# The rest of a weight block: a negated copy and an adding transfer in place of a subtraction

## The chip, the cores and the metric

The kernel runs on one core of a Trainium2 chip. The metric is the device time of one execution in microseconds (us), as the median of the runs shown. The core's engines are named as the profile names them: PE is TensorE (matrix products; PEld is its weight load), ACT is ScalarE, DVE is VectorE, POOL is GpSimd, and SP is SyncE, which here only issues transfers. SBUF is the on-chip memory, PSUM the eight banks that matrix products accumulate in, HBM the main memory.

## The reference

One layer of a hybrid decoder on 512 tokens of width 1024, in float32: a short convolution branch and a gated delta rule run side by side and are merged, then comes a gated feed-forward part with a convolution. Cut to what matters here, it is a row of products with large weight matrices, with cheap work on vectors between them:

```python
h = rmsnorm(x, norm_mix_g)
proj = h @ w_in                                   # 1024 x 9232
bg, cg, xv, q, k, v, z, a, b, ga, gb = split(proj)
y_a = (bg * causal_dwconv(cg * xv, conv_a_w)) @ w_a_out
y_b = gdn_branch(q, k, v, z, a, b, ...) @ w_b_out # chunked gated delta rule, 8 heads
x = x + (sigmoid(ga) * y_a + sigmoid(gb) * y_b) @ w_o
h = rmsnorm(x, norm_ffn_g)
up = causal_dwconv(h @ w_up, ffn_conv_w)          # 1024 x 5632
gate, val = split(up)
x = x + (silu(gate) * val) @ w_down               # 2816 x 1024
return rmsnorm(x, norm_final_g)
```

## The kernel before, in words

**Products in two parts.** Every float32 operand of a large product is split into a rounded part in the format float32r ("high", `wh` for weights) and the rest ("low", `wl`), which is the operand minus its rounded part. A product is then three products in float32r: high by high, high by low, low by high. `mm3` (L112) issues the three for the eight 128-row pieces of an input: in the kernel before, first `wh` by the input's low part and `wl` by its high part in turn, and the eight of high by high last. `row_jobs` (L912) does the same for `w_o` and `w_down`, where tokens lie on the output's partitions; there the order within each 128-row piece is low input by `wh`, high input by `wl`, high by high.

**Blocks and jobs.** All weights come as 81 blocks of 1 MB: 128 partitions by 8 pieces of 256 columns (`cols`), or by 2 rows of 1024 columns (`rows`, for `w_o` and `w_down`). A `Block` (L122) has three tiles from the pool `wp`, each in two buffers: `raw`, which `load` fills with one transfer that SP issues (L131), and `wh` and `wl`, which `split` makes. In the kernel before `split` works in pieces of 128 x 512: ACT copies a piece of `raw` into `wh` (L143), and DVE subtracts `wh` from `raw` into `wl` (L144); four pieces make a block.

**Order of the work.** `run_jobs` (L148) walks a list of jobs, one a block. While the products of job i are written out, the split of block i + 1 stands in the queue `splits`; `tick` (called after every four products of 512 columns) takes a step of it and of the queues `chains`, `mids`, `backs` (the stages of the delta rule) and `evacs` (what takes results out of PSUM). Block i + 2 is loaded meanwhile. A new `wh` or `wl` needs the buffer of the block two before, so it can't be written until the last product that reads that one. The framework then sets the order on each engine, and inserts the waits.

**The list.** 16 jobs for q, k, v and z of four pairs of heads, with the delta rule between their products; 4 for gb; 12 for cg, xv and bg; 4 for ga; 4 of `w_a_out`; 4 of `w_b_out`; 4 of `w_o`; 22 of `w_up`; 11 of `w_down`. A job of 256 columns is 48 products of 512 columns. In `row_jobs` the last two blocks are used together: the last but one is used for one or two of the four token groups alone, the rest waits for the last block. The first two blocks of `w_up` are used together as well (`first_val`), by halves of the tokens, in products of 256 columns; before them `fin1` forms the norm (with a power on POOL, L979) and PE turns the result.

**POOL** has little to do in the kernel before: constants, the polynomial of the decay gates (L426 to L443), powers (`sk` L511, `fac` L724, `r` L979 and L1075), a mask of the decay matrix (`Dm` L393), a product with a mask (`um` L538) and copies (`TTf` L616). It runs in order, as every engine does.

## Time and profile before

| | |
|---|---|
| runs shown | 1001.76, 1000.38, 999.54 us; median 1000.38 us |
| profiled execution, first to last instruction (span) | 998.5 us |
| median less span | 1.9 us |
| granted TensorE clock, mean | 0.999 |
| instructions in the span | 14009 |

The profiled execution has its span alone as its own time; the runs also count what lies ahead of the first and behind the last instruction, and the median is 1.9 us above this span. Rows of the trace give the start in us from the span's start, the duration, the engine, the line of the kernel, the operation, output and inputs, and a count where rows were merged; in square brackets stands how long the engine had been idle and who ended it. Products are pipelined: each one is shown for some 0.39 us, and the next one starts 0.23 us after it. A group's row gives busy time, mean duration in ns, and the idle time ahead of it.

### The profile page before, as it was taken

To read this page: it belongs to the slowest core of one execution; us is meant where nothing else is said; L and a number is where in the kernel's file an instruction comes from. 1 tells how busy PE (TensorE), PEld (TensorE's weight loads), DVE (VectorE), ACT (ScalarE), POOL (GpSimd) and SP (SyncE) were. 2 spreads that over 40 slices of the span, in tenths; PEclk is the share of its full clock that TensorE was granted. 3 is DMA by queue.
4 is the path that set the end of the run, shared out by engine and by line. 5 is a ranking of instruction groups with operands and counts; after the bars stand their busy time and mean duration, and the time that the engine had idled before them with its cause. 6 is when DMAs were issued, how large, how long until landed. Compare 5 with 4: busy or idle time off the path is not lost.

```text
span 998.5 us, 14009 instructions
## 1 busy us (share of the span) xinstructions
PE 986.6 (99%) x5602; PEld 822.5 (82%) x5602; DVE 545.8 (55%) x1090; ACT 426.2 (43%) x931; POOL 64.3 (6%) x101
## 2 busy tenths in 40 slices
PE   8999999999999999999999999999999999999997
PEld 5887888888888888888888888988888888888886
DVE  6777776897434434542253553675665666532235
ACT  6695666665353322322331232454444444421123
POOL 3331201202010000000000000000000000000000
PEclk9999999999999999999999999999999999999999
DMA  7343232232212232223223252332223223223212
GB/s 223 105 133 94 72 93 86 72 93 57 88 44 85 85 119 93 85 87 124 85 88 124 85 190 84 106 117 96 85 90 121 85 86 126 85 87 124 84 43 85
DMA packets 95409, 97.60 MB, mean 98 GB/s; under 512 B 20299, under 2 KB 88176, under 8 KB 95344
## 3 DMA queue, kind: packets, MB, share of 16 engines
q1 hardware_dynamic: 95344, 96.70, 30.3%
q8 instruction: 44, 0.72, 0.3%
q14 instruction: 21, 0.17, 0.1%
HBM read 93.27 MB, written 3.42 MB: 97 GB/s over the span
## 4 chain that ended last, share of the span: by engine, by line
PE 96%; DVE 1%; issue 1%; ACT 1%; DMA 0%; SPq 0%; POOL 0%; POOLq 0%; ACTq 0%
PE ps L104 88%; PE ps L484 1%; PE ps L519 1%; PE ps L713 1%; PE ps L693 1%; PE ps L702 1%; PE ps L681 1%; PE ps L680 1%; PE ps L656 0%; PE ps L650 0%; DMA raw<-in_w_in_dram 0%; PE ps L991 0%; ACT hT L341 0%; PE ps L603 0%; PE ps L594 0%
## 5 line engine op out<-in xcount | busy, mean ns | idle before, releaser
L104 PE MATMUL ps<-hT,wh 128*128 128x512 f32 (+1 forms) x1184 | 371.2, 391 | 0.3 <-ACT wh L143 0.3
L144 DVE TENSOR_TENSOR wl<-raw,wh 128x512 fp32r<-128x512 f32 x324 | 211.7, 692 | 160.5 <-ACT wh L143 160.1
L104 PEld LDWEIGHTS ps<-hT,wh 128*128 128x128 f32 x1184 | 218.0, 188 | 41.1 <-ACT wh L143 0.6
L143 ACT CAST wh<-raw 128x512 fp32r<-128x512 f32 x324 | 178.6, 618 | 170.5 <-PE ps L104 162.3
L104 PE MATMUL ps<-hT,wl 128*128 128x512 f32 (+1 forms) x592 | 227.0, 385 | 0.3 <-DVE wl L144 0.3
L104 PE MATMUL ps<-h,wh 128*128 128x512 f32 (+1 forms) x768 | 220.8, 372 | 0.0
L104 PEld LDWEIGHTS ps<-h,wh 128*128 128x128 f32 x768 | 140.1, 188 | 24.9
L104 PE MATMUL ps<-h,wl 128*128 128x512 f32 (+1 forms) x384 | 140.2, 371 | 0.0
L104 PEld LDWEIGHTS ps<-hT,wl 128*128 128x128 f32 x592 | 111.4, 188 | 20.5 <-DVE wl L144 0.5
L104 PE MATMUL ps<-wh,aT 128*128 128x512 f32 x352 | 108.5, 389 | 0.0
L104 PEld LDWEIGHTS ps<-h,wl 128*128 128x128 f32 x384 | 72.3, 188 | 12.5
L104 PEld LDWEIGHTS ps<-wh,aT 128*128 128x128 f32 x352 | 66.1, 188 | 13.7
L104 PE MATMUL ps<-wl,aT 128*128 128x512 f32 x176 | 68.5, 389 | 0.0
L188 DVE SCALAR_TENSOR_TENSOR cv<-ps,wA,cv 128x511 f32<-128x511 f32 (+2 forms) x72 | 53.5, 743 | 11.2 <-ACT cv L185 10.4
L188 DVE SCALAR_TENSOR_TENSOR g<-ps,wF,g 128x511 f32<-128x511 f32 (+1 forms) x44 | 32.9, 747 | 48.2 <-ACT g L185 47.9
L188 DVE SCALAR_TENSOR_TENSOR v<-ps,wF,v 128x511 f32<-128x511 f32 (+1 forms) x44 | 32.8, 747 | 34.6 <-ACT v L185 34.3
L104 PE MATMUL ps<-wh,mix 128*128 128x512 f32 x128 | 40.1, 391 | 0.0
L104 PE MATMUL ps<-ya,wh 128*128 128x512 f32 x128 | 39.6, 389 | 0.0
L104 PE MATMUL ps<-yb,wh 128*128 128x512 f32 x128 | 39.6, 389 | 0.0
L104 PEld LDWEIGHTS ps<-wl,aT 128*128 128x128 f32 x176 | 33.0, 188 | 6.9
L185 ACT ACTIVATE g<-ps,wF 128x512 f32<-128x512 f32 x22 | 15.2, 690 | 38.9 <-PE ps L104 38.9
L185 ACT ACTIVATE v<-ps,wF 128x512 f32<-128x512 f32 x22 | 15.2, 690 | 38.6 <-PE ps L104 38.6
(227 smaller groups left out, 970.0 us busy)
## 6 DMA issues: line engine op xcount, KB each, us to landing
raw<-in_w_in_dram SPq DMA_DIRECT2D x36, 1024.0 KB, 5.1
raw<-in_w_up_dram SPq DMA_DIRECT2D x22, 1024.0 KB, 5.1
raw<-in_w_down_dram SPq DMA_DIRECT2D x11, 1024.0 KB, 4.9
raw<-in_w_a_out_dram SPq DMA_DIRECT2D x4, 1024.0 KB, 5.7
raw<-in_w_b_out_dram SPq DMA_DIRECT2D x4, 1024.0 KB, 5.6
raw<-in_w_o_dram SPq DMA_DIRECT2D x4, 1024.0 KB, 6.7
Dm<-gtd SPq DMA_DIRECT2D x4, 512.0 KB, 3.9
x<-in_x_dram SPq DMA_DIRECT2D x4, 512.0 KB, 6.8
```

Of the source, the lines that this page charges most:

```text
L104: pe.matmul(o, lhsT=a, rhs=b, start=start, stop=stop)
L143: act.copy(out=self.wh[sl], in_=self.raw[sl])
L144: dve.tensor_tensor(out=self.wl[sl], in0=self.raw[sl], in1=self.wh[sl].bitcast(F32), op=ALU.subtract)
L185: act.activation(out=dst, in_=src, func=AF.Copy, scale=wcol(taps - 1))
L188: dve.scalar_tensor_tensor(out=dst[:, sh:], in0=src[:, :S - sh], scalar=wcol(j), in1=dst[:, sh:], op0=ALU.mult, op1=ALU.add)
L484: pe.transpose(out=o[:, n * P:(n + 1) * P], in_=src[:, n * P:(n + 1) * P], identity=ident)
L519: pe.matmul(o[:, i], lhsT=kqs[:, a, h, 0, sl], rhs=kqs[:, b, h, :, sl], start=a > 0, stop=a + b == 0)
L680: pe.matmul(o[:, 0:P], lhsT=kq[:, h, 0, sl], rhs=St[h], start=True, stop=True)
L681: pe.matmul(o[:, P:2 * P], lhsT=kq[:, h, 1, sl], rhs=St[h], start=True, stop=True)
L693: pe.matmul(o[:, 0:P], lhsT=TTf[:, f, :], rhs=rs[h], start=True, stop=True)
L702: pe.matmul(o2[:, 0:P], lhsT=kn[:, f, :], rhs=vns[h], start=True, stop=True)
L713: pe.matmul(o[:, 0:P], lhsT=A[:, f, :], rhs=vns[h], start=True, stop=True)
```

## The change

`split` makes two pieces of 128 x 1024 a block. For the first two blocks (`here`) it still subtracts on DVE. For the other 79, ACT copies the piece into `wh`, then writes minus `wh` into `wl` (L148), and POOL issues a transfer (L149) that reads the piece of the weight from HBM a second time and adds it onto `wl` in SBUF. These are 158 transfers of 512 KB. `mm3` and `row_jobs` issue what needs `wl` last, and `run_jobs` drains the queue `splits` ahead of the call that finishes a block's split, not behind it. Comments were taken out, so lines behind L143 shift by up to four (L393 is L396, L538 is L541, L724 is L727).

```diff
     def mm3(o, pairs, order=KO):
         n = len(pairs)
         pairs = [pairs[k] for k in order]
         for i, (ah, al, bh, bl) in enumerate(pairs):
-            mm(o, ah, bl, i == 0, False)
-            mm(o, al, bh, False, False)
+            mm(o, ah, bh, i == 0, False)
+        for ah, al, bh, bl in pairs:
+            mm(o, ah, bl, False, False)
         for i, (ah, al, bh, bl) in enumerate(pairs):
-            mm(o, ah, bh, False, i == n - 1)
+            mm(o, al, bh, False, i == n - 1)
...
-        def split(self):
+        def split(self, here=False):
             a, b = self.a, self.b
             if self.wh is not None:
                 return
             self.wh = wp.tile([P, a, b], F32R, tag="wh", name=nm("wh"))
             self.wl = wp.tile([P, a, b], F32R, tag="wl", name=nm("wl"))
-            h = max(1, 512 // b)
-            for a0 in range(0, a, h):
-                for b0 in range(0, b, 512):
-                    sl = (slice(None), slice(a0, min(a, a0 + h)), slice(b0, min(b, b0 + 512)))
-                    act.copy(out=self.wh[sl], in_=self.raw[sl])
+            for a0 in range(0, a, a // 2):
+                sl = (slice(None), slice(a0, a0 + a // 2))
+                act.copy(out=self.wh[sl], in_=self.raw[sl])
+                if here:
                     dve.tensor_tensor(out=self.wl[sl], in0=self.raw[sl], in1=self.wh[sl].bitcast(F32),
                                       op=ALU.subtract)
-                    yield
+                else:
+                    act.mul(out=self.wl[sl], in_=self.wh[sl].bitcast(F32), mul=-1.0)
+                    nc.gpsimd.dma_start(out=self.wl[sl], in_=self.src()[sl], accum_op=ALU.add)
+                yield

     def run_jobs(jobs):
         jobs[1][0].load()
         for i, (block, use) in enumerate(jobs):
+            drain(splits)
             Task(block.split()).finish()
-            drain(splits)
             if i + 1 < len(jobs):
-                splits.append(Task(jobs[i + 1][0].split()))
+                splits.append(Task(jobs[i + 1][0].split(i == 0)))
...
-            ks = Task(k_block.split())
+            ks = Task(k_block.split(True))
             norm_x(2)
             ks.step()
             scale_x(2)
             norm_x(3)
-            ks.step()
             scale_x(3)
             ks.finish()
...
-                for kk in range(2):
-                    k = 2 * g + kk
-                    xh, xl = x_[0][:, k, ts_], x_[1][:, k, ts_]
-                    mm(acc[t][hf], xl, wh[:, kk, hs], k == 0, False)
-                    mm(acc[t][hf], xh, wl[:, kk, hs], False, False)
-                    mm(acc[t][hf], xh, wh[:, kk, hs], False, k == nk - 1)
+                xs_ = [(kk, x_[0][:, 2 * g + kk, ts_], x_[1][:, 2 * g + kk, ts_]) for kk in range(2)]
+                for kk, xh, xl in xs_:
+                    mm(acc[t][hf], xh, wh[:, kk, hs], 2 * g + kk == 0, False)
+                    mm(acc[t][hf], xl, wh[:, kk, hs], False, False)
+                for kk, xh, xl in xs_:
+                    mm(acc[t][hf], xh, wl[:, kk, hs], False, 2 * g + kk == nk - 1)
```

Three places show what moves. Behind each name stands the number that the program gives a buffer. The first is POOL's order from the end of the gate polynomial (`g`) to the second mask of the decay matrix, before:

```order
L443 TENSOR_SCALAR g_420<-g_420 128x32 [waits Pool_49]
L511 TENSOR_TENSOR sk_644<-sk_644,phalf 128x8 [waits DVE_49]
L393 AFFINE_SELECT Dm_627<-Dm_627 128x1024 [waits DMAHW2_49]
L538 TENSOR_TENSOR um_755<-U_645,mask_106 32x256 [waits DVE_49]
L393 AFFINE_SELECT Dm_766<-Dm_766 128x1024 [waits DVE_49,DMAHW7_49,Activation_49,Pool_49]
```

And the same stretch now, from `g` on:

```order
L446 TENSOR_SCALAR g_414<-g_414 128x32 [waits Pool_49]
L149 DMA wl_500<-in_w_in_dram 128x4x256 [waits PE_49,Activation_49]
L149 DMA wl_500<-in_w_in_dram 128x4x256 [waits Activation_49]
L149 DMA wl_576<-in_w_in_dram 128x4x256 [waits PE_49,Activation_49]
L149 DMA wl_576<-in_w_in_dram 128x4x256 [waits Activation_49]
L396 AFFINE_SELECT Dm_617<-Dm_617 128x1024 [waits DMAHW2_49]
L514 TENSOR_TENSOR sk_634<-sk_634,phalf 128x8 [waits DVE_49]
L149 DMA wl_778<-in_w_in_dram 128x4x256 [waits DMASW0_49,DMASW1_49,PE_49,Activation_49]
L149 DMA wl_778<-in_w_in_dram 128x4x256 [waits Activation_49]
L541 TENSOR_TENSOR um_743<-U_635,mask_106 32x256 [waits DVE_49]
```

The adding transfers for the third and fourth job (`wl_500`, `wl_576`) stand behind the gate polynomial, and the mask product `um` and later masks stand behind those for the fifth.

The second place is ACT between the third job (v of the first pair) and the fourth (z): the eight sums of squares that become `ssk` (L504, now L507), before:

```order
L504 ACTIVATE junk_642,ssk_640<-ps_647 128x128 [waits PE_49]
L185 ACTIVATE cv_682<-ps_576,wA 128x512 [waits PE_49]
L504 ACTIVATE junk_642,ssk_640<-ps_647 128x128 [waits Activation_49] x3
L504 ACTIVATE junk_642,ssk_640<-ps_667 128x128 [waits PE_49,Activation_49]
L504 ACTIVATE junk_642,ssk_640<-ps_667 128x128 [waits Activation_49] x3
L766 ACT_TABLE_LOAD
L766 ACTIVATE vT_704<-cv_682 128x512 [waits DVE_49]
```

And now, where the exponentials of the decay matrix (`Dm`), a table load, the values (`vT`) and an evacuation (`cv_773`) stand among them:

```order
L507 ACTIVATE junk_632,ssk_630<-ps_637 128x128 [waits Activation_49] x3
L507 ACTIVATE junk_632,ssk_630<-ps_655 128x128 [waits PE_49,Activation_49]
L404 ACTIVATE Dm_617<-Dm_617,negG 128x128 [waits Pool_49]
L404 ACTIVATE Dm_617<-Dm_617,negG 128x128 x7
L507 ACTIVATE junk_632,ssk_630<-ps_655 128x128 [waits Activation_49]
L769 ACT_TABLE_LOAD
L769 ACTIVATE vT_692<-cv_670 128x512 [waits DVE_49]
L507 ACTIVATE junk_632,ssk_630<-ps_655 128x128 [waits Activation_49]
L189 ACTIVATE cv_773<-ps_660,wA 128x512 [waits PE_49]
L507 ACTIVATE junk_632,ssk_630<-ps_655 128x128 [waits Activation_49]
```

The last sum of squares has moved from ahead of the values to behind the evacuation of the third job's second half.

The third place is PE at the start of a block of `w_down` (`aT` is its input), before, where the second product reads `wl`:

```order
L104 MATMUL ps_7513<-wh_7645,aT_5905 128x512 [waits Activation_49]
L104 MATMUL ps_7513<-wl_7646,aT_5904 128x512 [waits DVE_49]
L104 MATMUL ps_7513<-wh_7645,aT_5904 128x512
L104 MATMUL ps_7513<-wh_7645,aT_5905 128x512 [waits Activation_49]
L104 MATMUL ps_7513<-wl_7646,aT_5904 128x512 [waits DVE_49]
```

And now:

```order
L104 MATMUL ps_7367<-wh_7843,aT_5798 128x512 [waits Activation_49]
L104 MATMUL ps_7367<-wh_7843,aT_5799 128x512
L104 MATMUL ps_7367<-wh_7843,aT_5798 128x512 [waits Activation_49]
L104 MATMUL ps_7367<-wh_7843,aT_5799 128x512
L104 MATMUL ps_7367<-wl_7844,aT_5798 128x512 [waits DMASW2_49]
L104 MATMUL ps_7367<-wl_7844,aT_5798 128x512 [waits DMASW3_49]
```

The fifth and sixth product now wait for the two adding transfers, four products (some 0.9 us) into the block. In a block of 256 columns it is the 17th and the 19th.

## The prediction

> **What bounds the kernel now.** I read the page first, its busy times, its chain and its groups:
>
> ```profile
> span 998.5 us, 14009 instructions
> PE 986.6 (99%) x5602; PEld 822.5 (82%) x5602; DVE 545.8 (55%) x1090; ACT 426.2 (43%) x931; POOL 64.3 (6%) x101
> ...
> PE 96%; DVE 1%; issue 1%; ACT 1%; DMA 0%; SPq 0%; POOL 0%; POOLq 0%; ACTq 0%
> ...
> L144 DVE TENSOR_TENSOR wl<-raw,wh 128x512 fp32r<-128x512 f32 x324 | 211.7, 692 | 160.5 <-ACT wh L143 160.1
> ...
> L143 ACT CAST wh<-raw 128x512 fp32r<-128x512 f32 x324 | 178.6, 618 | 170.5 <-PE ps L104 162.3
> ```
>
> PE is busy 99% of the span and 96% of the chain is PE. DVE's 211.7 us of subtractions, which the change removes, lie beside it; ACT waits 162.3 us for PE to free `wh`. Then the chain in order of time; its longest unbroken stretch but one is
>
> ```profile
> 316.16 303.79 PE ps L104 x1340
> ```
>
> 303.79 / 1340 = 0.227 us a product, so a job of 48 takes 10.9 us. No product is removed; the pace stays. A gain can come only from places where PE idles, a loss only where the new `wl` comes too late.
>
> Next the transfers:
>
> ```profile
> q1 hardware_dynamic: 95344, 96.70, 30.3%
> raw<-in_w_down_dram SPq DMA_DIRECT2D x11, 1024.0 KB, 4.9
> Dm<-gtd SPq DMA_DIRECT2D x4, 512.0 KB, 3.9
> x<-in_x_dram SPq DMA_DIRECT2D x4, 512.0 KB, 6.8
> ```
>
> 30.3% of 998.5 us for 96.70 MB is 3.13 us of all 16 DMA engines per MB, or 3.28 us for a block of 1024 KB.
>
> **The change part by part.**
>
> *DVE, ACT, POOL in total.* DVE loses 324 subtractions (211.7 us) and gets four of twice the size back, some 5 us. On ACT a row of a `w_down` block shows four casts in 2.19 us:
>
> ```profile
> 905.01 2.19 ACT L143 CAST wh<-raw 128x512 fp32r<-128x512 f32 x4 [8.70 <-PE ps L104]
> 905.67 2.50 DVE L144 TENSOR_TENSOR wl<-raw,wh 128x512 fp32r<-128x512 f32 x4 [8.38 <-ACT wh L143]
> 908.20 11.25 SPq L131 DMA_DIRECT2D raw<-in_w_down_dram  x2
> ```
>
> That is 0.53 us from start to start, so 1.06 us for a piece of 1024, and I price the negation alike: 4.2 us a block for 2.2, or about 165 us more, 59% of the span. PE hides that, save where ACT is full (below). POOL gets 158 issues. The shared DMA engines carry 79 blocks more: 79 x 3.28 = 259 us (26% of the span) if an add costs what a plain transfer does, 52% if it costs double, since it must also read what it adds to.
>
> *An add of 512 KB.* No trace of before shows one. To landing: at least 3.9 us (the 512 KB row), at most 6.8 (the other one); I take 5.1, between them, near a plain 1024 KB. In DMA engine time: 1.64 us at plain price, 3.28 at double. A speed below the plain one has no reason here, so no gain lies in it.
>
> *Start.* The first block's pieces are twice as large, and DVE scales `x` behind the first of them:
>
> ```profile
> 14.02 0.67 ACT wh L143
> 14.71 0.03 DVE wl L144
> 14.75 0.57 issue
> 15.32 0.75 DVE xr L326
> 16.22 0.41 PE ps L331 x2
> ```
>
> The cast grows by 0.5 us and the subtraction by 0.6; DVE waited little of it before, so the turn at 16.22 us comes about **0.9 us later**, and all behind it. The high products that now come first don't help: only four stand ahead of the turn.
>
> *Third job.* Its adds stand on POOL behind the gate polynomial:
>
> ```profile
> 39.36 0.29 POOL L443 TENSOR_SCALAR g<-g 128x32 f32<-128x32 f32 x1
> 45.40 0.14 PE ps L447 x2
> ```
>
> L447 stands 12 products into the job, and `wl` is wanted 4 products and 0.9 us of small ones later, at 47.2 us. The start shifts both POOL's end and this alike. From 39.65 to 47.2 are 7.6 us for the first add; the second has 8.0 and shares the engines. With 5.1 us for one and 3.3 more for the other it lands 8.4 us on: **0.3 us** late (0 to 1.6).
>
> *ACT from 45 to 70 us.* The window, then three rows of it:
>
> ```profile
> 50.00:75.00 25.00, 25.00 (x131) 21.10 (x130) 19.35 (x57) 23.43 (x65) 8.82 (x7) 1.00 0.44 133
> 47.45 1.28 ACT L455 ACT_TABLE_LOAD   x1
> 57.16 2.46 ACT L401 ACTIVATE Dm<-Dm,negG 128x128 f32<-128x128 f32 x8 [0.68 <-POOL Dm L393]
> 60.14 0.60 PE L484 MATMUL ps<-ident,kq 128*128 128x128 f32 x4
> ```
>
> ACT is busy 23.43 of 25 us, with 2 us a block to come. In the new order it has, from the third job's start (45.40 less 12 products, 0.9 later: 43.6): a cast and `kqs` 1.4, an evacuation 0.7, two negations 2.1, three table loads 3.8 among small work of 1.7: 53.3. Then sums and an evacuation, 2.6; `Dm` 2.46; a table load 1.28, `vT` 0.6, an evacuation 0.7 and three sums 1.4: the last sum of squares ends at about 62.3. `kn` (L505, 0.7) waits for it: 63.0. It frees the bank for PE's second turn in the fourth job, which stood at 60.14 and now comes 0.9 and six products later, at 62.4: **0.6 us** (0 to 2). On POOL `um` waits behind the adds, which wait for ACT's negations; nobody wants it for some 25 us.
>
> *The one stall of before.* DVE was late for `fac`:
>
> ```profile
> 195.24 1.64 POOL L724 TENSOR_TENSOR fac<-fac,nhalf 128x8 f32<-128x8 f32 x1 [7.89 <-DVE fac L723]
> 197.25 0.53 PE L484 MATMUL ps<-ident,vs 128*128 128x128 f32 x2 [0.74 <-DVE vs L732]
> ```
>
> With DVE freed it goes, with the products' hidden latency: **-0.9 us**; the product stream is next.
>
> *Blocks of `w_o` and `w_down`.* `wl` is wanted in the fifth product. Counted at 905 us: `wh` is free two products earlier than before (904.6), two casts and a negation end at 907.8, the second at 908.8; the next `raw` leaves at 906.7, when the casts end (SP waited for the subtraction before, to 908.20). Landing takes 4.9 us, 1.6 over its 3.28 of engine time; so the engines end both adds at 906.7 + 1.6 + 3.28 + 2w = 911.6 + 2w, and PE wants them at 905.0 + 10.9 + 0.9 = 916.8. It holds to w = 2.6; at 3.28 each block is 1.4 us late. I take 0.2 for each of 13 blocks: **2.6 us** (0 to 18).
>
> *The last block of each.* It has less time, as the job ahead is short. In `w_down`:
>
> ```profile
> 970.29 2.18 ACT L143 CAST wh<-raw 128x512 fp32r<-128x512 f32 x4 [8.70 <-PE ps L104]
> ```
>
> The order lets PE run 27 products (6.1 us) before `wl`; the first add leaves 2.9 us in, and with 3.9 to 5.1 lands at 6.8 to 8.0: 1.3 us. In `w_o`, 28 products (6.3): 1.2. Together **2.5 us** (1 to 5).
>
> *From `w_o` to `w_up`.*
>
> ```profile
> 623.69 2.19 ACT L143 CAST wh<-raw 128x512 fp32r<-128x512 f32 x4 [1.31 <-PE ps L104]
> 629.82 0.28 PE L104 MATMUL ps<-h,wh 128*128 128x256 f32 x1
> 629.94 0.28 PE L104 MATMUL ps<-h,wl 128*128 128x256 f32 x1
> ```
>
> From the cast to the first product are 6.1 us, then 16 narrow products of 0.12: `wl` is wanted 8.0 us in. Casts and a negation take 3.2, the add 5.1: 8.3; the second half, `w_up`'s second and third blocks the like. **2.0 us** (0 to 3.5). POOL's powers for the norm (L979) stand among these adds, which could delay PE's turns too.
>
> *Elsewhere* a block of 256 columns has `wl` wanted 16 products in: the second negation ends some 3 us into the job ahead, the add has over 11 us. That slack hides it; without it each job would grow.
>
> The sum: 0.9 + 0.3 + 0.6 - 0.9 + 2.6 + 2.5 + 2.0 = **+8.0 us**. Against its own time, the span, that is 1006.5; the median of the runs lies 1.9 us above the span: 1000.4 + 8.0 = **1008.4 us**. With the low ends 1001.4, with the high ends 1031.
>
> **A rule of the Trainium skill against it.** The row above gives 3.28 us for a block moved once. The Trainium skill's page Collectives: The Full Stack, section The bandwidth ceiling: the fold count and why AG ≠ RS ≠ AR, says that an add in the DMA costs two source reads, and so about halves the rate; no run of before can show it here. By that rule w is 3.28, the row blocks cost 18.2 us in place of 2.6, and the sum would be +23.6, or 1024.0 us, still inside this case.
>
> **The rivals.**
>
> *No net change.* If adds cost the plain 1.64 us and land in 3.9, only the start and the last blocks remain, and the freed DVE pays for them: within 2 us, 1000.4. For it: PE's 99% and 11 us of slack in most jobs. Against: the short windows above, which need no slow add.
>
> *Faster.* DVE is the mechanism, in the first 225 us: if its freed time (over 10% of each 25 us) removes more than the one stall, for PE also idles 0.3 to 0.7 us at waits in the start and loses some 1.7 us around 189 to 200. All of it gone gives 2.7 us: 997.7. It decides once adds land in under 4 us and ACT keeps up; ACT's 23.43 of 25 us speaks against it.
>
> *The adds set the pace.* A wide job lasts 10.9 us, its `raw` takes 3.28 of the engines, so at more than 3.8 us an add (2.3 times plain), or 5.4 us of POOL for an issue, every one of the 65 jobs behind the delta rule grows. At 2.5 times 11.5 us a job, +39: 1039; at three times +144: 1145. For it: an add reads, reads and writes, and POOL's price of an issue stands in no row. Against: DMA engines idle at 70% now.
>
> **How the numbers follow.** The forecast case (late at named places, 1002.4 to 1031) gets 0.52, no change 0.20, faster 0.08, the adds as the pace 0.20. About 2 us (0.2%) is what a measurement of this kernel can tell from no change. So faster 0.08, same 0.20, slower 0.72. The range runs from 998 to 1045: below it 0.05 is left out, above it about 0.13, the pace case's worse part.
>
> **What would show it.** Right: PE idle before `wl` with an add's landing as the reason, at 47, 590, 630 and 970 us and in `w_down`'s blocks; none in the jobs of 316 to 550 us; landings of 4 to 7 us; DVE near 340 us busy, ACT near 590; the turn at 17.1 us. Wrong: every job longer than 10.9 us (the pace), or no wait for `wl` anywhere and a span under 1000.

## The result, and the profile after

The changed kernel takes 1059.37 us (median of 4 runs, 1056.15 to 1061.97) against 1000.01 us before (4 runs, 999.54 to 1001.76): a ratio of 1.0588, 95% interval 1.0565 to 1.0611. It is slower, as forecast, but by 59 us in place of 8, and outside the range. The profiled execution has a span of 1054.4 us, 55.9 more than before; its mean granted clock is 0.977.

The page of the kernel after: span and busy times, the queues, the chain, two of the new groups, and one kind of new transfer.

```profile
span 1054.4 us, 14068 instructions
PE 1006.0 (95%) x5602; PEld 833.5 (79%) x5602; DVE 357.6 (34%) x770; ACT 557.3 (53%) x927; POOL 248.1 (24%) x259
...
q0 software_dynamic: 71904, 82.85, 48.8%
q1 hardware_dynamic: 95344, 96.70, 29.5%
...
PE 74%; DMA 12%; DVE 4%; issue 4%; ACT 3%; POOL 1%; SPq 1%; POOLq 0%; ACTq 0%; DVEq 0%
...
L148 ACT ACTIVATE wl<-wh 128x1024 fp32r<-128x1024 f32 x158 | 159.5, 1050 | 0.0
...
L149 POOL DMA_DIRECT2D wl<-in_w_in_dram x68 | 88.4, 1391 | 237.1 <-ACT wl L148 214.6
...
wl<-in_w_in_dram POOLq DMA_DIRECT2D x68, 512.0 KB, 7.4
```

PE's share of the chain fell from 96% to 74%, and 12% of it is now DMA. The software queue's packets took 48.8% of 1054.4 us for 158 adds, 3.26 us each, 1.9 times what half a block of `raw` takes (29.5% for 96.70 MB is 3.22 us per MB, 1.69 for 512 KB): near the upper of the two bounds in the prediction (3.28). The packets of the adds overlap, as the rates at e8 show, and by those rates an add takes less. An add from `w_in` lands 7.4 us after its issue (median), later than the longest landing assumed (6.8).

What PE waited for, by releaser (total us, times, longest):

```profile
PE ps L597 <- DMA T<-tbd: 12.2, 2, 10.0
PE ps L104 <- DMA wl<-in_w_o_dram: 6.6, 2, 3.6
PE ps L104 <- DMA wl<-in_w_up_dram: 5.2, 3, 2.0
PE ps L104 <- DMA wl<-in_w_down_dram: 4.4, 5, 2.3
PE ps L487 <- DVE kn L508: 3.3, 1, 3.3
```

The longest wait is for a tile that the change doesn't touch: `T`, the inverse factors in the delta rule. Before, no wait for it stood among PE's waits. The second row to the fourth are the waits for `wl` that were forecast.

Where the time went is read from landmarks, the starts of the first products of a kind in the trace (us). Runs e2, e3 and e12 are explained below; they belong in one table.

| stage (from, to) | before | after | e2: adds from block 16 | e3: adds in the middle | e12: mended |
|---|---|---|---|---|---|
| start, to the product on `g` (L447, now L450) | 45.2 | 47.1 | 46.8 | 46.2 | 48.2 |
| delta rule and on: from there to the first product on `ya` | 452.2 | 479.0 | 463.3 | 462.9 | 456.7 |
| `w_a_out` and `w_b_out`: `ya` to `mix` | 87.0 | 87.0 | 87.1 | 87.0 | 87.1 |
| `w_o`: `mix` to `h` | 45.4 | 57.1 | 57.3 | 45.4 | 45.4 |
| `w_up`: `h` to `aT` | 242.4 | 251.1 | 251.2 | 242.4 | 242.3 |
| `w_down`: first to last product of `wh` on `aT` | 119.4 | 125.8 | 126.7 | 119.0 | 119.0 |

So 26.8 us were lost between the start and `ya`, 11.7 in `w_o`, 8.7 at the handover to `w_up` and in its first blocks, 6.4 in `w_down`, and nothing in the jobs between. The start lost 1.9 us here; but among profiled executions of the kernels below whose code is the same up to there this landmark lies anywhere from 45.7 to 49.3 us, so that a single one tells it to a few us only.

### The profile page after: what moved, and what is told of

It is laid out like the page before. It is cut to its first block, busy times and chain, and to the rows that moved or that the text cites. A ratio compares the mean times of both kernels' runs of the same rounds, so it can differ in the third digit from the quotient of the medians.

```text
span 1054.4 us, 14068 instructions
## 1 busy us (share of the span) xinstructions
PE 1006.0 (95%) x5602; PEld 833.5 (79%) x5602; DVE 357.6 (34%) x770; ACT 557.3 (53%) x927; POOL 248.1 (24%) x259
## 3 DMA queue, kind: packets, MB, share of 16 engines
q0 software_dynamic: 71904, 82.85, 48.8%
q1 hardware_dynamic: 95344, 96.70, 29.5%
## 4 chain that ended last, share of the span: by engine, by line
PE 74%; DMA 12%; DVE 4%; issue 4%; ACT 3%; POOL 1%; SPq 1%; POOLq 0%; ACTq 0%; DVEq 0%
PE ps L104 68%; DMA wl<-in_w_down_dram 3%; DMA wl<-in_w_o_dram 2%; DMA wl<-in_w_up_dram 2%; DVE cv L192 1%; DMA Dm<-gtd 1%; ACT wh L143 1%; DMA T<-tbd 1%; PE ps L522 1%; PE ps L487 1%; DMA ucd<-U 1%; ACT wl L148 1%; DMA xt<-in_x_dram 1%; DMA UB<-ucd 1%; DMA tbd<-TB 1%
## 5 line engine op out<-in xcount | busy, mean ns | idle before, releaser
L104 PE MATMUL ps<-hT,wh 128*128 128x512 f32 (+1 forms) x1184 | 291.7, 393 | 1.7 <-ACT wh L143 1.4
L143 ACT CAST wh<-raw 128x1024 fp32r<-128x1024 f32 x162 | 163.1, 1050 | 194.2 <-PE ps L104 192.8
L104 PE MATMUL ps<-h,wh 128*128 128x512 f32 (+1 forms) x768 | 170.4, 375 | 0.0
L148 ACT ACTIVATE wl<-wh 128x1024 fp32r<-128x1024 f32 x158 | 159.5, 1050 | 0.0
L104 PE MATMUL ps<-hT,wl 128*128 128x512 f32 (+1 forms) x592 | 149.8, 393 | 0.0
L149 POOL DMA_DIRECT2D wl<-in_w_in_dram x68 | 88.4, 1391 | 237.1 <-ACT wl L148 214.6
L149 POOL DMA_DIRECT2D wl<-in_w_up_dram x44 | 57.2, 1472 | 180.1 <-ACT wl L148 179.9
L104 PE MATMUL ps<-h,wl 128*128 128x512 f32 (+1 forms) x384 | 89.3, 374 | 5.2 <-DMA wl<-in_w_up_dram 5.2
L104 PE MATMUL ps<-wh,aT 128*128 128x512 f32 x352 | 94.1, 390 | 0.0
L104 PE MATMUL ps<-wl,aT 128*128 128x512 f32 x176 | 55.9, 395 | 4.5 <-DMA wl<-in_w_down_dram 4.4
L192 DVE SCALAR_TENSOR_TENSOR cv<-ps,wA,cv 128x511 f32<-128x511 f32 (+2 forms) x72 | 53.5, 742 | 18.9 <-ACT cv L189 17.9
L192 DVE SCALAR_TENSOR_TENSOR v<-ps,wF,v 128x511 f32<-128x511 f32 (+1 forms) x44 | 32.9, 749 | 57.8 <-ACT v L189 57.1
L149 POOL DMA_DIRECT2D wl<-in_w_down_dram x22 | 18.9, 868 | 103.8 <-ACT wl L148 103.0
```

Source lines behind the costliest of these rows:

```text
L104: pe.matmul(o, lhsT=a, rhs=b, start=start, stop=stop)
L143: act.copy(out=self.wh[sl], in_=self.raw[sl])
L148: act.mul(out=self.wl[sl], in_=self.wh[sl].bitcast(F32), mul=-1.0)
L149: nc.gpsimd.dma_start(out=self.wl[sl], in_=self.src()[sl], accum_op=ALU.add)
L192: dve.scalar_tensor_tensor(out=dst[:, sh:], in0=src[:, :S - sh], scalar=wcol(j), in1=dst[:, sh:], op0=ALU.mult, op1=ALU.add)
```

## The experiments

"e1" means the run whose label begins so. The ratios are to the kernel before.

### Where the loss lies: e1 to e4

Each changes only which blocks are subtracted by DVE (`here`):

```diff
-                splits.append(Task(jobs[i + 1][0].split(i == 0)))
+                splits.append(Task(jobs[i + 1][0].split(True)))        # e1
+                splits.append(Task(jobs[i + 1][0].split(i < 15)))      # e2
+                ... not (16 <= i + 1 < 44 or 51 <= i + 1 < 70) ...     # e3
+                ... i == 0 or i >= 15 ...                              # e4
```

> All 81 blocks get their rest by DVE's subtraction, in two pieces of 128x1024, in the new order of products; no adding transfer and no negation is left. Theory (the adding transfers make the loss): within 2 us of the kernel before, 999 to 1003 us. Rival (the new order of products and the larger pieces make a part of it): over 1006 us, and the delta-rule stage longer than before without any add. DVE then does 162 subtractions of some 1.3 us, about as busy as before.

> Blocks 1 to 15 (the delta rule's jobs) by DVE's subtraction, blocks 16 to 80 by the adding transfer. Theory (the loss is made stage by stage: 28.7 us up to the end of the delta rule, 11.7 in w_o, 8.7 at the handover to w_up, 6.4 in w_down): 1000.0 + 26.8 = 1027 us, 1024 to 1032. Rival (the later stages' lateness depends on the first, or the loss of the first stage comes back later): under 1018 or over 1040.

> Adding transfers only in the column jobs away from the delta rule and the row blocks: blocks 16 to 43 and 51 to 69 (47 of 81 blocks); the others by DVE's subtraction. Theory (a column job wants the rest 16 products in, and that slack hides the add): within 4 us of the kernel before, 998 to 1004. Rival (every add costs something, such as by shared DMA engines or ACT's negations): 47/79 of the 59 us, so 1035; by half of that 1017.

> Adding transfers only for blocks 2 to 15, in the delta rule's stage (28 adds); all others by DVE's subtraction. Theory: 1000.0 + 28.7 = 1029 us, 1022 to 1032, with the landmark at which the first long unbroken stretch of products starts near 344 us. Rival (the loss in the first 345 us comes from the new order of products and piece sizes, not from the adds): near 1000 to 1006.

| run | us, median | ratio, 95% interval |
|---|---|---|
| e1, no add | 1014.69 | 1.0139, 1.0121 to 1.0157 |
| e2, adds from block 16 | 1041.63 | 1.0402, 1.0385 to 1.0418 |
| e3, 47 adding blocks in the middle | 1013.09 | 1.0119, 1.0102 to 1.0137 |
| e4, adds in the delta rule's jobs | 1028.08 | 1.0278, 1.0253 to 1.0303 |

The theory failed for e1: without any add the kernel is 13.2 us slower than before (1014.69 - 1001.51, the median before in that series). e2 and e3 missed their expected times by some 13 us, which they didn't reckon with, and e4 met its own only by luck: 28.7 us were expected of its adds, and 13.2 of them are there without any. Against e1 the parts add up: late adds +26.9 (e2), adds in the delta rule's jobs +13.4 (e4), the middle -1.6, inside the intervals (e3). 13.2 + 26.9 + 13.4 = 53.5 of the 59; the other 6 weren't traced. In the middle an add is indeed free: no stage of e3 behind the start is longer than in e1.

### The 13 us without any add: e5, e11, e13, e9

In e1 PE waits for `T` too, and the rows of the trace show why it is late. Here ACT and DVE in e1:

```profile
56.18 2.44 ACT L404 ACTIVATE Dm<-Dm,negG 128x128 f32<-128x128 f32 x8
...
58.89 1.28 ACT L769 ACT_TABLE_LOAD   x1
...
60.72 0.26 ACT L507 ACTIVATE junk<-ps 128x128 f32<-128x128 f32 x1
...
61.10 0.69 DVE L508 TENSOR_TENSOR kn<-ps,kdv 128x512 f32<-128x512 f32 x1 [1.33 <-ACT junk L507]
```

Before, ACT ended its sums of squares at 53.1 us, and `Dm`'s exponentials came behind them. In e1 the framework put the exponentials, a table load and the values `vT` ahead of the last sums, and `U`, which needs both, starts at 64.4 us, not 57.6. From there the chain `ucd`, `UB`, `TB`, `tbd`, `T` goes on late, and its steps on DVE now stand between the next pair's convolutions: from the first to the end of the last they take 16.8 us (74.0 to 90.8), 8.2 before (68.9 to 77.1). So `T` is issued at 94.84 us, not 79.63. The waits of e1:

```profile
PE ps L597 <- DMA T<-tbd: 4.3, 4, 3.5
PE ps L606 <- DVE TT L590: 1.8, 1, 1.8
```

e5 takes e1 and cuts the split in four pieces again, so that only the order of products is new (and, in the start, one step of the second block's split fewer ahead of the last scaling). e11 takes the kernel before and makes only its pieces larger. e13 is e1 with `T` used later in PE's queue, e9 is e1 with PE's wait filled:

```diff
-            for a0 in range(0, a, a // 2):                              # e5: e1 with
+            h = max(1, 512 // b)
+            for a0, b0 in [(a0, b0) for a0 in range(0, a, h) for b0 in range(0, b, 512)]:
...
-            h = max(1, 512 // b)                                        # e11: before with
-            for a0 in range(0, a, h):
-                for b0 in range(0, b, 512):
+            for a0 in range(0, a, a // 2):
...
-        for _ in range(Y_T):                                            # e13: e1 with
+        for _ in range(Y_T + (8 if pr == 0 else 0)):
...
         o = bank()                                                      # e9: e1 with
+        for _ in range(16 if pr == 0 else 0):
+            pe.matmul(o, lhsT=hT[0][:, 0, 0:P], rhs=hT[0][:, 0, :], start=True, stop=True)
         for f in range(8):
```

> As the kernel without adding transfers (1014.7 us), but the split goes back to four pieces of 128x512, so that only the new order of products differs from the kernel before. In that run PE waited for T at 96.7 us, since U, and with it the chain to T, came 6.8 us later than before. Theory (the new order of products does it: wh comes free earlier, so casts move ahead of the delta rule's work in ACT's queue, and exponentials and SiLUs alternate there with more table loads): 1010 to 1016 us, with the wait for T. Rival (the larger pieces do it, as each holds ACT and DVE twice as long): 999 to 1003, without that wait.

> The kernel before, with its split in two pieces of 128x1024 in place of four of 128x512, and nothing else. Theory (the size of the pieces is not what costs; the order of products is): 999 to 1004 us. Rival (either one disturbs the delta rule's front): 1008 to 1014, with a wait for T.

> The kernel without adding transfers (1014.7 us), with the first pair's T used 8 ticks (32 wide products, 7.3 us) later in PE's queue. Theory (each change of the product order or the piece size makes U and so T late, and that one wait with the slow clock behind it is the whole 12 to 13 us): 1001 to 1005, no wait for T. Rival (the late front costs in other ways too, such as the later pairs' chains): 1008 to 1014.

> The kernel without adding transfers (1014.7 us), with 16 more wide products (3.6 us, thrown away) in PE's queue just ahead of the first pair's products on T, where PE waited 3.5 us in that run and then ran at a granted clock of 0.50 from 98 to 110 us. Theory (the half clock follows from the idle time, and costs more than the wait): the products fill the wait, the clock stays at 1.0, and the time falls by 4 to 6 us, to 1009 to 1011, though work was added. Rival (the low clock comes from something else, or the wait alone is the loss): 1014 to 1018.

| run | us, median | ratio, 95% interval |
|---|---|---|
| e5, new order of products alone | 1012.05 | 1.0116, 1.0098 to 1.0134 |
| e11, larger pieces alone | 1012.47 | 1.0125, 1.0108 to 1.0142 |
| e13, no add, `T` used later | 1005.10 | 1.0038, 1.0024 to 1.0051 |
| e9, no add, wait for `T` filled | 1013.31 | 1.0130, 1.0116 to 1.0144 |

The order alone costs what the pieces alone cost, and both together hardly more: either one moves ACT's work in the first pair's front (`U` starts at 63.6 us in e5 and 63.3 in e11), and the same wait for `T` follows (its longest part is 3.5 us in e5, 3.9 in e11). e5's rival and e11's theory fell; "either one disturbs the front" holds. e13 shows that the wait is the cause of most of it: with `T` wanted later, 13.2 us over the kernel before become 3.9. These 3.9 weren't followed; in the trace the stretch from the product on `g` to `ya` is 3.1 us longer than before (455.3 us), 9.3 shorter than in e1.

e9 meant to show what the slow clock behind that wait costs. The clock did stay higher (0.50 from 98 to 110 us in e1, below 0.7 only from 104 to 108 in e9), and from the product on `g` to the chain's products at L653 (in e9 L655) it took 65.7 us (48.60 to 114.32) in place of 68.4 (45.70 to 114.13), with 3.6 us of products added. But the median fell by 1.4 us only, to 1013.31, against the kernel before of each series by 0.2 us, and the two intervals overlap: the runs don't confirm the theory.

### The adds in the delta stage: e6, e14, e15, e17

The steps of the first pair's chain, by the starts of the issues on SP's queue. First the kernel before, where PE wants `T` at 90.7 us:

```profile
60.81 2.75 SPq L533 DMA_DIRECT2D ucd<-U  x4
64.83 0.83 SPq L535 DMA_DIRECT2D UB<-ucd  x2
77.31 0.84 SPq L574 DMA_DIRECT2D tbd<-TB  x2
79.63 2.00 SPq L579 DMA_DIRECT2D T<-tbd  x4
```

Then the kernel after, with PE's first product on `T`:

```profile
49.17 0.33 SPq L466 DMA_DIRECT2D gtd<-GT  x1
53.89 0.35 SPq L395 DMA_DIRECT2D Dm<-gtd  x1
71.71 3.16 SPq L536 DMA_DIRECT2D ucd<-U  x4
81.47 1.00 SPq L538 DMA_DIRECT2D UB<-ucd  x2
101.63 1.00 SPq L577 DMA_DIRECT2D tbd<-TB  x2
105.36 1.78 SPq L582 DMA_DIRECT2D T<-tbd  x4
...
109.56 0.59 PE L597 MATMUL ps<-T,um 32*32 32x32 f32 x6 [10.02 <-DMA T<-tbd]
```

`Dm` can leave once `gtd` has landed, `UB` once `ucd` has: 4.7 and 9.8 us, in e1 2.2 and 3.1. Three causes were possible: the shared DMA engines, ACT's negations, POOL's queue. e14 and e17 keep DVE's subtraction and issue the same adds into a part of `yb` that isn't in use yet; e15 has the negations alone; e6 leaves the changed kernel as it is but uses `T` later:

```diff
                 if load:                       # e14: e1 with this, for blocks 2 to 9; e17: blocks 4 to 9
+                    act.mul(out=t[:, 0, 0:1], in_=self.wh[:, a0, 0:1].bitcast(F32), mul=-1.0)
+                    nc.gpsimd.dma_start(out=t, in_=self.src()[sl], accum_op=ALU.add)
...
+                    act.mul(out=t, in_=self.wh[sl].bitcast(F32), mul=-1.0)   # e15, blocks 2 to 9
...
-        for _ in range(Y_T):                                                # e6: after with
+        for _ in range(Y_T + (12 if pr == 0 else 0)):
```

> The changed kernel, with the first pair's T used 12 ticks (48 wide products, 10.9 us) later in PE's queue; nothing else. Theory (PE's wait of 10.0 us for T at 100 us, and the clock at half speed behind it, are the largest part of the delta stage's loss): the wait is gone, and the time falls by 10 to 18 us, to 1041 to 1049. Rival (T is only the first of a row of late results, and the next one, such as the scan or the second pair's front, takes over the wait): 1053 to 1060.

> The kernel without adding transfers, in which POOL issues for blocks 2 to 9 the same two adding transfers of 512 KB a block as the changed kernel does, but into a part of yb that nobody uses yet, behind a one-column negation on ACT; wl still comes from DVE. Nobody waits for these transfers; they are traffic alone. Theory (in the delta stage the adds cost by holding the shared DMA engines, so that the small transfers gtd, Dm, ucd, UB, tbd and T land later): 1022 to 1034 us, T wanted but 8 to 12 us away. Rival (it is ACT's negations and POOL's waits): 1013 to 1017.

> The kernel without adding transfers, in which ACT makes the negated copy of blocks 2 to 9 (two of 128x1024 a block), into the same unused part of yb; no adding transfer, wl from DVE. Theory (shared DMA engines): 1014 to 1018, as ACT's 2.1 us a block find room. Rival (ACT's negations hold the front back): 1022 or more.

> As the run with traffic alone, but for blocks 4 to 9 only: there the unused adds of blocks 2 and 3 stood on POOL ahead of the gate polynomial, and gtd left 6.0 us later than without adds, which is no matter of the DMA engines. Theory (shared DMA engines slow the small transfers from Dm on): gtd leaves within 2 us of 48.9, the steps from ucd to UB, UB to TB and T's landing are longer by 8 to 11 us together, and the time is 1020 to 1028 against 1014.7 without traffic. Rival (the 18 us of that run were POOL's): 1013 to 1017.

| run | us, median | ratio, 95% interval |
|---|---|---|
| e6, after, `T` used later | 1045.60 | 1.0450, 1.0423 to 1.0477 |
| e14, unused adds, blocks 2 to 9 | 1032.77 | 1.0317, 1.0299 to 1.0335 |
| e15, unused negations | 1011.84 | 1.0110, 1.0091 to 1.0130 |
| e17, unused adds, blocks 4 to 9 | 1025.94 | 1.0260, 1.0242 to 1.0277 |

The negations cost nothing (e15 against e1: -2.9 us). Twelve adds that nobody waits for cost 11.3 us (e17 against e1). In e17 `gtd` leaves within 0.6 us of where it does in e1, and then:

```profile
49.49 0.33 SPq L473 DMA_DIRECT2D gtd<-GT  x1
51.83 0.35 SPq L402 DMA_DIRECT2D Dm<-gtd  x1
68.20 2.29 SPq L543 DMA_DIRECT2D ucd<-U  x4
76.00 0.87 SPq L545 DMA_DIRECT2D UB<-ucd  x2
96.09 0.86 SPq L584 DMA_DIRECT2D tbd<-TB  x2
99.82 2.46 SPq L589 DMA_DIRECT2D T<-tbd  x4
```

From `ucd` to `UB` are 7.8 us (3.1 in e1), from `UB` to DVE's first step on it 5.7 (3.3; it starts at 81.7), from `T`'s issue to its first product 4.6 (1.9): 9.8 us of transfers of 32 KB that land late. The medians from issue to landing agree: `ucd` 6.5, `UB` 4.8 and `T` 5.1 us in e17, 2.4, 2.9 and 2.0 in e1. The Trainium skill's page DMA: Bandwidth & Descriptors, section Queues, rings and completion order, says that each DMA engine goes round the queues that have work, a packet at a time; a small transfer then shares with a large one of another queue. That the small ones are slowed and not stopped agrees; at what grain, no run here shows.

e14's larger loss has POOL's queue in it: there the adds of blocks 2 and 3 stood ahead of the gate polynomial, and `gtd` left at 54.95 us. e6 answers for the changed kernel: `T`'s wait fell from 12.2 to 1.2 us and the time by 13.8 us, about half of the stage's 26.8. The other half stays in e6 (466.0 us from `g` to `ya`, 452.2 before); PE waits there 3.8 us for `kn` and 2.2 for the scan's `r`, and the rest wasn't followed.

### What an add costs, and what slack hides it: e8, e10

e8 takes the add out of the transfer; e10 goes back to the old order in `mm3`, so that `wl` is wanted in the second product of a wide job:

```diff
-                    nc.gpsimd.dma_start(out=self.wl[sl], in_=self.src()[sl], accum_op=ALU.add)
+                    nc.gpsimd.dma_start(out=self.wl[sl], in_=self.src()[sl].bitcast(F32R))   # e8
...
-            mm(o, ah, bh, i == 0, False)                                                      # e10
-        for ah, al, bh, bl in pairs:
-            mm(o, ah, bl, False, False)
+            mm(o, ah, bl, i == 0, False)
+            mm(o, al, bh, False, False)
         for i, (ah, al, bh, bl) in enumerate(pairs):
-            mm(o, al, bh, False, i == n - 1)
+            mm(o, ah, bh, False, i == n - 1)
```

> The changed kernel, with each adding transfer replaced by a plain one of the same bytes from the same queue to the same place and with the same waits (wl then holds the weights themselves: the add is left out). Theory (what the adds cost is their time on the shared DMA engines, 3.26 us for 512 KB, twice a plain transfer): the software queue's share falls to about half (24 to 26%), the row blocks' and the handover's losses (26.8 us) fall to under 8, the delta stage's loss over the kernel without adds (13.4) to about half: 1000 + 13 + 7 + 8 = 1028 us (1020 to 1035). Rival (the cost lies in what stands before the add, the negation on ACT and the issue on POOL): within 5 us of 1059.

> The changed kernel, adds and all, with the order of products in the wide jobs as before (both small products of each pair first, the large ones last); the row blocks as in the changed kernel. Theory (that order cost the 11.8 us that the run with small pieces shows, all in the delta stage): 1047 us (1043 to 1052). Rival (the new order is what gives the adds their time: in the old one wh comes free 8 products, 1.8 us, later and wl is wanted 15 products, 3.4 us, earlier, against some 4.4 us of slack in the wide jobs at 417 us of the changed kernel): the wide jobs wait for wl, and the time is 1060 or more.

e8: 1025.54 us, 1.0261 (1.0237 to 1.0286), near the 1028 of the theory. Of the 26.8 us of `w_o`, the handover and `w_down` 5.9 are left, of the delta stage's loss over e1 5.2 (469.8 us against 464.6), and PE still waits 8.8 us for `T`. The software queue's share fell to 36.8% of 1024.4 us, 2.39 us a transfer, not to half as expected. POOL's issue became shorter too (from `w_in` 1391 to 755 ns), so e8 alone doesn't part the two. The rate shows the price better: stretches of 1 us in the middle of the list, in which the two transfers of a block run and next to nothing else (busy times, clock, DMA share, GB/s), in the kernel after, and the like in e8:

```profile
412.00:413.00 1.00, 1.00 (x7) 0.80 (x6) 0.69 (x1) 0.22 (x1) 0.00 (x0) 1.00 1.21 186
413.00:414.00 1.00, 1.00 (x6) 0.84 (x5) 0.57 (x1) 0.40 (x1) 0.00 (x0) 1.00 1.24 200
```

```profile
413.00:414.00 1.00, 1.00 (x6) 0.81 (x6) 0.00 (x0) 0.28 (x1) 0.00 (x0) 1.00 1.79 363
```

With all engines busy, adds bring in 186 to 200 GB/s, plain transfers of the same queue 363. At these rates 512 KB take 2.6 to 2.8 us as an add and 1.4 as a plain transfer. The packets' times add up to 1.2 and 1.8 of the engines' time there (the last column but one), so they overlap, and the queue's share overstates the price. That an add about halves the rate, as the section named in the prediction says of a reduction between cores (Collectives: The Full Stack, the Trainium skill), these traces bear out.

e10: 1137.22 us, 1.1372 (1.1350 to 1.1394). Its rival held. PE's waits there:

```profile
PE ps L104 <- DMA wl<-in_w_in_dram: 32.2, 24, 3.8
PE ps L104 <- DMA wl<-in_w_up_dram: 25.0, 18, 5.3
```

With those for `w_a_out` (3) and `w_b_out` (3) they are 48 waits over 64 such blocks. So the wide jobs hid their adds only by the new order: by it `wl` is wanted 3.4 us later, and `wh` comes free 1.8 us earlier. The DMA engines aren't full in e10 (busy 0.72 to 0.91 of each 25 us from 400 to 500 us), so what a job waits for seems to be the way from a free `wh` over casts and negation to the landed add; no run parts these.

### The row blocks and the clock: e7, e16, e18

e7 puts the products on `wl` of a row block behind all its others (but in the last block); e16 puts 13 products by zeros ahead of the first ones on `wl` in the second and fourth block of `w_o`; e18 writes the loads of `gff` and `x1` behind the second block of `w_o`:

```diff
-                for t in range(NT):                                  # e7
-                    part(g, t)
+                for o in (0, 1):
+                    for t in range(NT):
+                        part(g, t, (o,))
...
+                for _ in range(13 if nk == ND and g in (1, 3) and t + hf == 0 else 0):     # e16
+                    pe.matmul(acc[t][hf], lhsT=st["zero"], rhs=wh[:, 0, hs], start=False, stop=False)
                 for kk, xh, xl in xs_:
                     mm(acc[t][hf], xh, wl[:, kk, hs], False, 2 * g + kk == nk - 1)
...
+                if early and g == 1:                                 # e18
+                    load_x1()
```

> The changed kernel, with the products on wl put behind all others of a block in the row blocks of w_o and w_down (all blocks but the last of each), so that wl is wanted 32 products (7.3 us) into a block in place of 4 (0.9 us). Theory (an add of 512 KB lands 1 to 4 us after PE wants it there, and each such wait is followed by products at half speed): the waits inside w_down and the first in w_o go, those before the two last blocks stay: 10 us less, 1049 (1045 to 1053). Rival (the row blocks are slow because the DMA engines fall behind steadily): the wait only moves and the time stays within 3 us of 1059.

> The changed kernel, with 13 products by a matrix of zeros (3.0 us, they add nothing) ahead of the first products on wl in the second and the fourth block of w_o, where PE waited 3.0 and 3.6 us and the granted clock then was 0.50. Theory (the half clock follows from PE's idle time and costs about 5 of the 11.7 us that w_o lost): the clock stays at 1.0 there, w_o takes 51 to 53 us in place of 57.1, and the kernel 1053 to 1056. Rival (the clock falls for another reason, or the added products cost what the clock gives): w_o takes 57 us or more, the kernel 1058 to 1062.

> The changed kernel, with the loads of gff and x1 (2.5 MB, by the queue that carries raw) moved from the start of w_o behind its second block. In the changed kernel the DMA engines are full from 614 to 638 us, and the run with products by zeros showed that w_o's length (57.1 us, 45.4 before) is set by the time at which the adds land, not by PE. Theory (these loads and the adds share the engines, and the adds land later by it): the second block's wait of 3.0 us goes, w_o takes 51 to 54 us, the kernel 1053 to 1056. Rival (raw and the adds alone fill the engines): w_o within 1.5 us of 57, the kernel 1057 to 1061.

| run | us, median | ratio, 95% interval | `w_o`, us | `w_down`, us |
|---|---|---|---|---|
| after | 1059.37 | 1.0588, 1.0565 to 1.0611 | 57.1 | 125.8 |
| e7 | 1052.16 | 1.0511, 1.0475 to 1.0546 | 53.9 | 123.3 |
| e16 | 1059.86 | 1.0587, 1.0566 to 1.0608 | 57.9 | 126.5 |
| e18 | 1054.91 | 1.0556, 1.0533 to 1.0579 | 57.0 | 126.3 |

e7 brought 7.2 us of the 10 expected: the waits inside `w_down` went (4.4 us in 5 became 2.3 in one, that of the last block), and so did the one in the second block of `w_o`, but at the last block of `w_o` PE now waits 5.5 us (3.6 in the kernel after).

e16 splits in two. In the second block the theory held. The kernel after, PE's rows:

```profile
624.92 0.39 PE L104 MATMUL ps<-wl,mix 128*128 128x512 f32 x1
628.31 0.79 PE L104 MATMUL ps<-wl,mix 128*128 128x512 f32 x1 [3.00 <-DMA wl<-in_w_o_dram]
628.90 1.91 PE L104 MATMUL ps<-wh,mix 128*128 128x512 f32 x4
```

Four products start over 1.70 us, 0.43 each. In windows of 2 us the granted clock (last column but two) of the kernel after is then:

```profile
628.00:630.00 2.00, 1.69 (x4) 1.41 (x5) 0.00 (x0) 0.00 (x0) 0.81 (x1) 0.50 1.02 420
...
632.00:634.00 2.00, 2.00 (x6) 1.54 (x5) 0.00 (x0) 0.00 (x0) 0.00 (x0) 0.50 0.97 204
634.00:636.00 2.00, 2.00 (x9) 1.64 (x8) 0.00 (x0) 0.00 (x0) 0.00 (x0) 0.90 1.12 239
```

In e16 the same place reads:

```profile
621.90 3.11 PE L932 MATMUL ps<-wh,zero 128*128 128x512 f32 x13
624.85 0.39 PE L104 MATMUL ps<-wl,mix 128*128 128x512 f32 x1
626.22 0.50 PE L104 MATMUL ps<-wl,mix 128*128 128x512 f32 x1 [0.98 <-DMA wl<-in_w_o_dram]
626.55 1.09 PE L104 MATMUL ps<-wh,mix 128*128 128x512 f32 x4
```

The wait is 0.98 us, the clock stays at 1.00, and the block's sixth set of `wh` products starts 11.0 us after its first (620.99 to 632.02) in place of 12.9 (624.01 to 636.95), with 3.0 us of products added. So the half clock follows from the idle time, and there it cost about as much again as the wait (without filling and wait the stretch in e16 is 11.0 - 3.0 - 1.0 = 7.0 us; 12.9 - 3.0 - 7.0 = 2.9). In the fourth block the gain was lost: its second add landed 9.2 us after its issue, PE waited 1.3 and 1.9 us, and the clock fell to 0.50 after all. `w_o` as a whole is as long as it was. From the product that waited last for these adds to `h` are 18.8 us in e16 (649.26 to 668.04) and 19.1 in the kernel after (651.15 to 670.25): the end follows the landing of the last adds, and what PE gained ahead of it is lost in the wait. The rival's number held.

e18 didn't do what it was for. SP reached those loads at 612.37 us, right behind the third `raw`, as in the kernel after (614.05 with `w_o` starting 1.6 us later), since nothing holds them there. `w_o` stayed at 57.0 us; that the median lies in the theory's range is no support for it, and its interval overlaps that of the kernel after. Whether the 2.5 MB beside the adds make them late is open. The trace of the kernel after speaks for it: the two adds of the second block, issued beside these loads, landed after 9.7 and 12.5 us, those of the first block after 7.3 and 8.9, of the third after 8.6 and 10.6, of the last after 7.1 and 8.6.

### Everything mended: e12

The changed kernel with e7's order, `T` used 12 ticks later, and DVE's subtraction for 13 of the 79 blocks:

```diff
-                splits.append(Task(jobs[i + 1][0].split(i == 0)))
+                splits.append(Task(jobs[i + 1][0].split(not (8 <= i + 1 < 45 or 51 <= i + 1 < 80))))
```

> The changed kernel with every place of loss found so far mended and 66 of the 79 adds kept: DVE's subtraction for blocks 2 to 7 (beside the first pair's chain), 45 to 50 (w_o but its first block, and the first three of w_up) and 80 (the last of w_down); the first pair's T used 12 ticks later; wl last in the row blocks. Theory (the loss of 59 us is made up of these places and nothing else): 1005 us (1000 to 1010). Rival (the adds also cost something everywhere, or what is mended in one place comes back in another): 1015 or more.

1010.26 us, 1.0091 (1.0075 to 1.0107), against 1059.4: five sixths of the loss went with 66 adds kept. It lies 0.3 us above the theory's range and 4.7 below the rival's. In the table above its stages from `ya` on are as before. What remains in its trace is 3.0 us in the start, within the spread of that landmark, and 4.5 in the delta rule, where adds still run. No version run here is faster than the kernel before.

## Why the prediction was right in direction and wrong in size

**Start, +0.9.** Not to be told from the spread: 0.5 to 4.1 us over the kernel before's one trace at the product on `g`. The turn that was to come at 17.1 us came at 16.7 in the kernel after.

**Third job, +0.3.** Within its 0 to 1.6: no wait for `wl` at 47 us stands in the trace.

**ACT from 45 to 70 us, +0.6. This step failed, and it is the largest miss.** It followed `kn` and `um` and said of `um` that nobody wants it for 25 us. `kn` cost 3.3 us, not 0.6. But the longer chain through `U`, `ucd`, `UB`, `TB` to `T` wasn't followed: before, `T` was issued from 79.63 us on, landed 3.5 to 3.8 us after each issue and was wanted at 90.7, and some 6 to 7 us of slack were all it had. The new order and the larger pieces used up more than that by themselves (`T` issued 15 us later in e1; 12 to 13 us of time in e5, e11 and e1, most of it gone in e13), and the adds delayed the chain's small transfers by 10 more (e17). The step priced the adds as somebody's wait for `wl`, never as traffic beside the delta rule's own transfers. The sum of that stage was 0.0 behind the start; it measured 26.8, of which the wait for `T` is about half (e6); the rest is known in part only.

**The one stall of before, -0.9.** Wrong: `PE` still waits 0.7 us for `vs` (L735) there, though DVE is busy 357.6 us and not 545.8. The freed DVE bought no time.

**Blocks of `w_o` and `w_down`, 2.6, and the last of each, 2.5.** The mechanism and the places were right, the size was off: 11.7 + 6.4 = 18.1 us. It would be easy to blame w: at 3.28, near the 3.26 of the queue's share, the prediction's own arithmetic gives 18.2 + 2.5 = 20.7. But that it comes near is luck, for it puts 1.4 us on each of 13 blocks, and the inner blocks of `w_down` waited only three times, 0.40 to 0.55 us each: 1.4 us for ten blocks, where the sum had 2.0. The rates agree with these: an add of 2.6 to 2.8 us stands at the threshold of 2.6. What failed is the landing: in the last blocks it was taken as 3.9 to 5.1 us, and the two adds took 7.1 and 8.6 in `w_o`, 5.5 and 7.2 in `w_down`. PE waited 3.6 and 3.0 us there for 1.2 and 1.3. Also mis-sized is the second block of `w_o`, 3.0 us for 0.2, where the step didn't count the 2.5 MB loaded beside the adds; that these are the reason is not shown. And behind both waits of `w_o` the granted clock was 0.50, which the sum didn't have; in `w_down` it stayed at 1.00.

**The handover, 2.0.** Right place, mis-sized: 8.7 us, through the same landing (7.6 us from `w_up`, median): 5.2 us of waits, and half the clock behind the first two of the three.

**Elsewhere, 0.** Right: 87.0 us from `ya` to `mix` in both, e3's 47 blocks free. But e10 shows that it rested on the order of the products: without the 3.4 and 1.8 us that this order gives, most jobs grow. The rival of the adds as the pace had another condition, more than 3.8 us of the engines for an add or 5.4 us of POOL, and neither came: 2.6 to 3.26 us, and 1.39.

The forecast case got its name right (late at named places) and its end wrong: with the high ends of its terms it reached 1031. The places that it named for late weights lost 26.8 us, about as much as their high ends together (18 + 5 + 3.5); the other 26.8 came from a place that it had at nothing. So the direction was right for half of its reason.

## What to carry to other kernels

Before a transfer is added under a compute-bound stage, look for chains of small transfers that run there, and ask what slack their last consumer has: here the stage with a chain of 32 KB copies lost as much as all late weights together. Where a framework sets the order, a change in piece size or product order alone can move another chain by more than the change itself does; a run with the order changed and the new operation left out prices that. For a transfer of a new kind the time to landing is a term of its own: taken here from plain transfers as 5.1 us, it was 7 to 9 in most places, and the short windows turned on it.

## What the runs showed of the hardware that was not expected

An adding transfer keeps all DMA engines busy at 186 to 200 GB/s where a plain one of the same queue brings 363 (e8). POOL spends 1391 ns on an issue of an add from `w_in`, and 755 ns on a plain one of the same bytes (e8).

No length of a wait divides those with a half clock behind them from those without. In the kernel after every single wait of PE from 2.5 us up (at 67, 110, 218, 628 and 651 us) was followed by a granted clock of 0.50. The waits of 1.99 and 2.27 us (at 708 and 1031 us) weren't, though one of 2.17 us in e12 (at 198 us) was, and so were two close together of 1.27 and 1.92 (at 674 and 676). How long the low clock stays differs too: some 6 us behind the wait at 628 us, 3 behind that at 651, and 12 in e1. A short wait can so cost about twice its length.

Filling such a wait with idle products kept the clock up in the second block of `w_o` (e16), and gained nothing over `w_o` as a whole: a low clock behind a wait is not a loss of its own where the next operand is late anyway.
